# Od, gd and hg stores issued by the sync engine, and every second gd copy staged in a `wn` tile, in a hybrid encoder layer

## The chip, the cores and the metric

The kernel runs on one core of a Trainium2 chip. The metric is the device time of the whole program in microseconds (us): the median of several executions. The engines are TensorE (PE; PEld is its weight load), VectorE (DVE), ScalarE (ACT), GpSimd (POOL) and SyncE (SP). SP computes nothing here; it issues DMA transfers. ACT computes and issues transfers too. Every engine takes its own instructions in order.

## The reference

One layer of an encoder, for 2048 rows of 1024 columns. Cut to its core:

```python
u = rms_norm(h); proj = u @ w_in                   # 1024 -> Hyena, mLSTM, gate columns
hy = short_conv(proj[hyena columns])
y_hy = group_norm(hyena(hy, spectra of the sin-FFN filters))   # two FFT convolutions, gated
qk = silu(short_conv(proj[q, k columns]))
y_ml = group_norm(sigmoid(o_pre) * (mlstm(q, k, v, gates) + mlstm of the flipped rows))
h = h + concat(y_hy, y_ml) @ w_out
q, k, v = norm(h) @ wq, norm(mem) @ wk, norm(mem) @ wv         # mem: 256 rows
h = h + (softmax(q k^T / 16) v per head) @ wo                   # 4 heads of 256
h = h + square(relu(norm(h) @ w1)) @ w2                         # 1024 -> 4096 -> 1024
out = norm(h)
```

## The kernel before

All products are made in single precision by a split: each operand becomes a high and a low part, and `mm3` (L355) issues three matmuls, hi*hi, hi*lo and lo*hi. PE therefore has 14287 matmuls.

The program is written as Python generators, one for each part, and `program` (L2078) weaves them: it steps one generator or the other by the weights that they yield. The order so written goes to a tile framework, which lists the instructions for each engine anew by a timeline that it models (`schedule_with_timeline_sim`). So the order on an engine follows from the order of the code, from the tiles and from the modelled times. A tile is taken by a tag; a tag has a number of buffers (`bufs`), and a tile of the tag can only be written when what used that buffer is done. For a store that means that the data have left the tile.

Every DMA that SP or ACT issues counts on one of eight semaphores in turn, shared by both engines. An issuing instruction waits until the earlier DMA on its semaphore is complete, and then what stands behind it on its engine waits too.

The stages in time, with the generators that make them:

- 0 to some 1030 us: the input projection and the two FFT convolutions of Hyena. `sweep` makes column blocks whose rows are turned; `natural` (L856) makes the blocks of v (`c2` 0 and 1, stored to `vd`) and of the output gate (`c2` 2 and 3, stored to `od`), for each half `hf` of the rows, in eight tiles of 128 rows. After its matmuls a tile is copied by ACT (L885) or passed through a sigmoid by ACT (L887) into a tile `st` of three buffers, and stored (L888). The order of the blocks is: half 1 with blocks 3, 0, 1, 2; half 0 with block 3, later 0 and 1, and at the end block 2.
- some 1020 to 1180 us: `memproj` (L689), woven with the last Hyena transforms and the first mLSTM steps. It folds the attention's weights with the memory rows: `project` (L698) makes `kt`, 16 matmuls (L704) and a copy by ACT (L706); `keys` (L714) makes from `kt` and a weight four products of 128x512 (L721), and each goes through `staged` (L709), a copy by ACT (L711) into a tile `o` of the tag `st`, and a store to `gd` (L723); `values` (L725) does the like for `vw` (L733, L735). There are four `keys` and four `values`. The weights `wm` come through `raw_stream` (L417) on SP in tiles of the tags `wl` and `wh`. The Hyena tail beside it reads `zg` and `hy` (`a`, L963, L966), stores `yh` (L1058) and loads `cbn` (L1248), on SP.
- some 1180 to 1840 us: cross-attention (four chunks `c` of 512 rows), with the remaining mLSTM steps woven in. Its first PE work is L1460, transposes of `wn` tiles that hold `yh`. At the end of a chunk `store` (L1600) scales a block of the result by ACT (L1602) into `hg`, two buffers, and stores it to DRAM (L1603), eight for each chunk.
- from some 1840 us: the MLP, to the end.

An mLSTM step on PE is a chain: updates of the state (L1190), scores (L1274), sums over values and state (L1312 and L1314), with DVE and ACT work between them (L1196, L1284, L1326).

The tag `wn` in the pool of the first stages has four buffers. It holds weights as they land, before they are split (L396).

Of the kernel before, what the change touches and what calls it, by code (L numbers as in the profile page):

```python
# [10 lines left out]
F32 = mybir.dt.float32  # L11
# [122 lines left out]
class Prog:  # L134
# [554 lines left out]
    def memproj(self):  # L689
        nc, sb = self.nc, self.isb  # L690
        gd = self.dram("gd", (2, 128, 8, 512))
        vw = self.dram("vw", (4, 128, 8, 256))
        self.pop(2)
        mt = self.memt

        mul = nc.tensor.matmul

        def project():  # L698
            w = next(self.mst)
            p = self.mm().rearrange("p (k t) -> p k t", k=2)  # L700
            for m in range(2):
                ms = slice(128 * m, 128 * m + 128)
                for k in range(8):
                    mul(p[:, m], w[:, k, ms], mt[k // 4][:, k % 4], start=k == 0, stop=k == 7)  # L704
            t = sb.tile([128, 4, 256], F32, tag="xn", name="kt", bufs=2)[:, 0:2]
            nc.scalar.copy(t, p)  # L706
            return t

        def staged(p):  # L709
            o = sb.tile([128, 2, 256], F32, tag="st", name="o", bufs=3)  # L710
            nc.scalar.copy(o, p)  # L711
            return o

        def keys(h, t):  # L714
            q = next(self.mst)
            for i2 in range(4):
                p = self.mm().rearrange("p (i t) -> p i t", i=2)
                for i in range(2):
                    ds = slice(256 * i2 + 128 * i, 256 * i2 + 128 * i + 128)
                    for m in range(2):  # L720
                        mul(p[:, i], q[:, m, ds], t[:, m], start=m == 0, stop=m == 1)  # L721
                cs = slice(256 * (h % 2), 256 * (h % 2) + 256)
                nc.scalar.dma_start(out=gd[h // 2, :, 2 * i2:2 * i2 + 2, cs], in_=staged(p))  # L723

        def values(h, t):  # L725
            o_ = next(self.mst)
            for mt in range(2):
                ms = slice(128 * mt, 128 * mt + 128)
                for d in range(2):
                    ds = slice(512 * d, 512 * d + 512)  # L730
                    p = self.mm()
                    for m in range(2):
                        mul(p, t[:, m, ms], o_[:, m, ds], start=m == 0, stop=m == 1)  # L733
                    o = staged(p.rearrange("p (i t) -> p i t", i=2))
                    nc.scalar.dma_start(out=vw[2 * d:2 * d + 2, :, 2 * h + mt].rearrange("i p c -> p i c"), in_=o)  # L735

        t = project()
        for i in range(8):
            yield 11
            nxt = project() if i < 7 else None  # L740
            (keys if i < 4 else values)(i % 4, t)
            t = nxt
# [113 lines left out]
    def natural(self, hf, tiles, after=None, at=4):  # L856
        nc, a, sb = self.nc, self.a, self.isb
        xh, xl = self.xh, self.xl
        win = a["w_in"][0]
        for c2 in tiles:  # L860
            n = 256 if c2 < 3 else 272
            c0 = 2560 + 256 * c2
            wh, wl = next(self.wst)
            for t in range(8):
                if t % 4 == 0:
                    yield 11
                if c2 == tiles[-1] and after is not None:
                    if after is True and t == 0:
                        nxt = self.x_chunks(0)
                    if t == at:  # L870
                        if after is True:
                            self.prepq = nxt
                        else:
                            after()
                ts = slice(128 * t, 128 * t + 128)
                r0 = 1024 * hf + 128 * t
                p = self.mm()
                for k in range(8):
                    self.mm3(p[:, :n], xh[:, k, ts], xl[:, k, ts], wh[:, k, :n], wl[:, k, :n], k == 0, k == 7)
                if self.pending:  # L880
                    self.pending.pop(0)()
                self.pop()
                so = sb.tile([128, 512], F32, tag="st", name="st", bufs=3)[:, 0:256]
                if c2 < 2:
                    nc.scalar.copy(so, p[:, :256])  # L885
                else:
                    nc.scalar.activation(so, p[:, :256], AF.Sigmoid)  # L887
                nc.scalar.dma_start(out=(self.d_vd if c2 < 2 else self.d_od)[r0:r0 + 128, 256 * (c2 % 2):256 * (c2 % 2) + 256],  # L888
                                  in_=so)
                if c2 == 3:  # L890
                    sg = sb.tile([128, 16], F32, tag="sg", name="sg", bufs=2)
                    nc.vector.tensor_tensor(sg, p[:, 256:272], self.gb, ALU.add)
                    nc.sync.dma_start(out=self.d_gt[r0:r0 + 128], in_=sg)
# [524 lines left out]
    def attention(self, es):  # L1418
        nc, tc, a = self.nc, self.tc, self.a
        ys = [self.dram("yh", (L, CH)), self.dram("ym", (L, CH))]  # L1420
        gd = self.dram("gd", (2, 128, 8, 512))
        vw = self.dram("vw", (4, 128, 8, 256))
        h2 = self.dram("h2", (4, 128, 8, 512))
        hgd = self.dram("hg", (4, 128, 8, 512))
# [20 lines left out]
        def gemm(w, i, r, p=None, ks=range(8)):  # L1445
            p = p or self.mm()
            ms = slice(128 * i, 128 * i + 128)
            for k in ks:
                self.mm3(p, w[0][:, k, ms], w[1][:, k, ms], r[0][:, k], r[1][:, k], k == 0, k == 7)
            return p  # L1450
# [32 lines left out]
        for c in range(4):  # L1483
# [19 lines left out]
            for ct in range(8):  # L1503
# [14 lines left out]
                if c == 0 and ct < 4:  # L1518
                    p = gemm(w, ct % 2, y, half[ct], range(4, 8))
                else:  # L1520
                    p = gemm(w, ct % 2, y)
# [10 lines left out]
            o = self.act()  # L1532
# [64 lines left out]
            def keep(ct, c=c):  # L1597
                nc.sync.dma_start(out=h2[c, :, ct - 3:ct + 1], in_=acc[:, ct - 3:ct + 1])

            def store(ct):  # L1600
                hg = A.tile([128, 512], F32, tag="hg", name="hg", bufs=2)
                nc.scalar.activation(hg, acc[:, ct], AF.Copy, scale=gf[:, ct:ct + 1])  # L1602
                nc.scalar.dma_start(out=hgd[c, :, ct], in_=hg)  # L1603
                if ct == 3 or (ct == 7 and c < 3):
                    keep(ct)

            for ct in range(8):
                yield 5.2
                if ct % 2 == 0:
                    w = next(wst) if ct else w  # L1610
                else:
                    k = sums.pop(0) if sums else None
                    if k is not None:
                        self.sums_x(A, k, "e")
                if c == 3 and ct in (1, 3, 5):
                    self.ffn_pre(ct // 2)
                if c == 3 and ct in (4, 6):
                    self.load_w1(ct // 2 - 2)
                if c == 3 and ct == 6:
                    x7 = self.ffn_xload(0, 7)  # L1620
                p = gemm(w, ct, o, half[ct], range(4, 8)) if ct < 2 else gemm(w, ct % 2, o)
                if prev is not None:
                    finish(ct - 1, prev, ssum)
                    store(ct - 1)
                prev = p
            if c == 3:
                self.ffn_x(7, x7)
            finish(7, prev, ssum)
            store(7)

            def stats(c=c, ssum=ssum):
# [539 lines left out]
```

## Time and profile before

| | us |
|---|---|
| three runs | 3091.53, 3103.35, 3098.87 |
| their median | 3098.87 |
| the profiled execution, its own time | 3097.53 |
| its span, first to last instruction | 3095.8 |
| mean granted PE clock of the span | 0.992 of full speed |

The profile page's list of DMA queues shows the two queues that hardware feeds, SP's (q1) and ACT's (q10), with packets, MB and the share of the 16 DMA engines' time:

```profile
q1 hardware_dynamic: 405988, 546.54, 55.1%
q10 hardware_dynamic: 37892, 57.79, 5.5%
```

In the prediction's windows the columns are the stretch in us from the start of the span, its length, the busy time of PE, PEld, DVE, ACT and POOL with the number of instructions, the PE clock that was granted (1.00 is full), the busy share of the DMA engines and GB/s. A line of waits has engine, tile, line, the arrow to what released it, the total in us, how many, and the longest. SPq and ACTq are the engines' DMA-issuing instructions. The line numbers are those of the kernel before; from the edit of `staged` on, the changed kernel's are larger by three.

### The profile page before, as it was taken

To read this page: it belongs to the slowest core of one execution; us is meant where nothing else is said; L and a number is where in the kernel's file an instruction comes from. 1 tells how busy PE (TensorE), PEld (TensorE's weight loads), DVE (VectorE), ACT (ScalarE), POOL (GpSimd) and SP (SyncE) were. 2 spreads that over 40 slices of the span, in tenths; PEclk is the share of its full clock that TensorE was granted. 3 is DMA by queue.
4 is the path that set the end of the run, shared out by engine and by line. 5 is a ranking of instruction groups with operands and counts; after the bars stand their busy time and mean duration, and the time that the engine had idled before them with its cause. 6 is when DMAs were issued, how large, how long until landed. Compare 5 with 4: busy or idle time off the path is not lost.

```text
span 3095.8 us, 42982 instructions
## 1 busy us (share of the span) xinstructions
PE 3023.0 (98%) x14287; PEld 2375.2 (77%) x14287; DVE 1952.6 (63%) x3442; ACT 1500.4 (48%) x2930; POOL 1130.9 (37%) x798
## 2 busy tenths in 40 slices
PE   9999999999999998999999999999999999999998
PEld 7655767776676766888887888888888888888876
DVE  8855465446656456877664666557555686566695
ACT  6443465534656225565544455556555543333335
POOL 0122011200222343333132237766466374244653
PEclk9999999999999999999999999999999999999999
DMA  6554767575867997464476556657544565353434
GB/s 225 187 191 164 243 214 237 178 234 193 260 199 241 301 309 231 151 204 160 149 246 222 183 188 224 210 180 240 196 153 151 183 212 171 109 166 117 159 102 164
DMA packets 444102, 607.07 MB, mean 196 GB/s; under 512 B 38494, under 2 KB 248542, under 8 KB 442856
## 3 DMA queue, kind: packets, MB, share of 16 engines
q1 hardware_dynamic: 405988, 546.54, 55.1%
q10 hardware_dynamic: 37892, 57.79, 5.5%
q8 instruction: 113, 1.85, 0.2%
q14 instruction: 109, 0.89, 0.1%
HBM read 401.79 MB, written 202.41 MB: 195 GB/s over the span
## 4 chain that ended last, share of the span: by engine, by line
PE 82%; DMA 7%; DVE 5%; ACT 2%; issue 2%; POOL 1%; SPq 0%; ACTq 0%; DVEq 0%; POOLq 0%
PE mm L357 17%; PE mm L361 17%; PE mm L360 17%; PE hy L357 6%; PE hy L361 6%; PE hy L360 6%; PE hy L178 3%; PE mm L948 2%; PE hy L979 1%; PE hy L1021 1%; DMA a<-hy 1%; DMA xt<-in_x_t_dram 1%; PE hy L1312 1%; PE mm L733 1%; PE hy L1314 1%
## 5 line engine op out<-in xcount | busy, mean ns | idle before, releaser
L1669 ACT CAST ah<-w 128x512 fp32r<-128x512 f32 x284 | 177.1, 624 | 302.0 <-PE hy L360 155.3
L1670 DVE TENSOR_TENSOR bl<-wr,bh 128x512 fp32r<-128x512 f32 x213 | 238.2, 1123 | 124.7 <-ACT bh L1669 124.7
L368 DVE TENSOR_TENSOR wl<-wn,wh 128x512 fp32r<-128x512 f32 (+1 forms) x296 | 215.4, 773 | 101.1 <-ACT wh L368 100.8
L1026 POOL TENSOR_TENSOR b<-b,a 128x512 f32<-128x512 f32 x64 | 86.8, 1359 | 510.5 <-ACT b L1024 240.8
L357 PE MATMUL mm<-xh,wh 128*128 128x512 f32 x640 | 265.5, 416 | 2.5 <-ACT st L206 1.3
L360 PE MATMUL mm<-xl,wh 128*128 128x512 f32 x640 | 252.9, 395 | 1.8 <-DVE xl L368 1.8
L361 PE MATMUL mm<-xh,wl 128*128 128x512 f32 x640 | 253.6, 397 | 0.0
L1670 DVE TENSOR_TENSOR al<-w,ah 128x512 fp32r<-128x512 f32 x236 | 216.4, 917 | 57.1 <-ACT ah L1669 56.9
L1669 ACT CAST bh<-wr 128x512 fp32r<-128x512 f32 x232 | 143.8, 622 | 223.6 <-PE mm L361 173.8
L361 PE MATMUL mm<-bh,al 128*128 128x512 f32 x576 | 223.7, 391 | 3.8 <-DVE al L1670 3.8
L357 PE MATMUL mm<-bh,ah 128*128 128x512 f32 x576 | 225.8, 392 | 0.8 <-DVE acc L1832 0.7
L360 PE MATMUL mm<-bl,ah 128*128 128x512 f32 x576 | 224.9, 390 | 0.0
L368 ACT CAST wh<-wn 128x512 fp32r<-128x512 f32 (+1 forms) x296 | 165.0, 619 | 104.6 <-PE mm L361 52.6
L360 PE MATMUL mm<-act,wh 128*128 128x512 f32 x512 | 201.8, 394 | 0.0
L361 PE MATMUL mm<-act,wl 128*128 128x512 f32 x512 | 199.3, 391 | 0.4 <-DVE wl L368 0.4
L357 PE MATMUL mm<-act,wh 128*128 128x512 f32 x512 | 198.7, 394 | 1.0 <-ACT wh L368 0.9
L357 PE MATMUL hy<-bh,ah 128*128 128x512 f32 x448 | 175.2, 391 | 0.0
L360 PE MATMUL hy<-bl,ah 128*128 128x512 f32 x448 | 174.6, 390 | 0.0
L361 PE MATMUL hy<-bh,al 128*128 128x512 f32 x448 | 174.4, 390 | 0.0
L357 PEld LDWEIGHTS mm<-xh,wh 128*128 128x128 f32 x640 | 120.1, 188 | 56.0 <-issue 19.2
L357 PE MATMUL mm<-wh,xh 128*128 128x256 f32 (+1 forms) x512 | 155.6, 304 | 3.5 <-ACT xh L368 2.0
L361 PEld LDWEIGHTS mm<-xh,wl 128*128 128x128 f32 x640 | 120.1, 188 | 46.2 <-issue 21.8
(380 smaller groups left out, 8219.6 us busy)
## 6 DMA issues: line engine op xcount, KB each, us to landing
wr<-hc SPq DMA_DIRECT2D x224, 256.0 KB
w<-in_ff_w_dram SPq DMA_DIRECT2D x172, 256.0 KB
hc<-wn SPq DMA_DIRECT2D x128, 256.0 KB
wn<-in_w_in_dram SPq DMA_DIRECT2D x100, 256.0 KB
hc<-q SPq DMA_DIRECT2D x96, 256.0 KB
fs<-a SPq DMA_DIRECT2D x32, 512.0 KB
a<-fs SPq DMA_DIRECT2D x64, 256.0 KB
a<-zs SPq DMA_DIRECT2D x64, 256.0 KB
```

The lines of the kernel that those rows point to most:

```text
L178: b = self.nc.tensor.matmul(*products[-1], start=True, stop=True)
L357: first = mm(ps, lh, rh, start=start, stop=False)
L360: mm(ps, lh, rl, start=False, stop=False)
L361: self.last = mm(ps, ll, rh, start=False, stop=stop)
L368: both = (self.nc.scalar.copy(hi, src), self.nc.vector.tensor_tensor(lo, src, hi.bitcast(F32), ALU.subtract))
L733: mul(p, t[:, m, ms], o_[:, m, ds], start=m == 0, stop=m == 1)
L948: nc.tensor.matmul(pp, dm[:, m], t[:, m], start=True, stop=True)
L979: nc.tensor.matmul(pg, em[:, m], y, start=True, stop=True)
L1021: nc.tensor.matmul(pp, dm[:, m], t[:, m], start=True, stop=True)
L1026: nc.gpsimd.tensor_tensor(xt, xt, hi[:, m], ALU.mult)
L1669: self.nc.scalar.copy(hi, src)
L1670: eng.tensor_tensor(lo, src, hi.bitcast(F32), ALU.subtract)
```

## The change

Three groups of stores are issued by `nc.sync` (SP) instead of `nc.scalar` (ACT): the `od` stores of column block 2 in `natural` (16), the `gd` stores of `keys` (16) and the `hg` stores of attention (32). The `od` stores of block 3, the `vd` stores and the `vw` stores stay on ACT. In `keys`, the copies of `i2` 0 and 2 go to a tile of the tag `wn` (four buffers), those of 1 and 3 to the tag `st` (three) as before. The bytes and the arithmetic are the same.

```diff
-        def staged(p):
-            o = sb.tile([128, 2, 256], F32, tag="st", name="o", bufs=3)
+        def staged(p, wide=False):
+            if wide:
+                o = sb.tile([128, 2, 256], F32, tag="wn", name="o", bufs=4)
+            else:
+                o = sb.tile([128, 2, 256], F32, tag="st", name="o", bufs=3)
             nc.scalar.copy(o, p)
             return o
...
-                nc.scalar.dma_start(out=gd[h // 2, :, 2 * i2:2 * i2 + 2, cs], in_=staged(p))
+                nc.sync.dma_start(out=gd[h // 2, :, 2 * i2:2 * i2 + 2, cs], in_=staged(p, i2 % 2 == 0))
...
-                nc.scalar.dma_start(out=(self.d_vd if c2 < 2 else self.d_od)[r0:r0 + 128, 256 * (c2 % 2):256 * (c2 % 2) + 256],
-                                  in_=so)
+                (nc.sync if c2 == 2 else nc.scalar).dma_start(
+                    out=(self.d_vd if c2 < 2 else self.d_od)[r0:r0 + 128, 256 * (c2 % 2):256 * (c2 % 2) + 256], in_=so)
...
-                nc.scalar.dma_start(out=hgd[c, :, ct], in_=hg)
+                nc.sync.dma_start(out=hgd[c, :, ct], in_=hg)
```

How the scheduler lists the instructions now, at the places that matter. First ACT in the keys' stage, before, with the semaphores that a row waits for (DMAHW0 to DMAHW7 are the eight DMA semaphores; a name like PE_49 is an engine's own):

```order
L723 DMA gd<-o 128x2x256 [waits DMAHW5_49,Activation_49]
L711 COPY o<-mm 128x512 [waits DMAHW3_49,PE_49]
L1184 ACTIVATE ve<-va,cols 128x129 [waits DMAHW7_49]
L1184 ACTIVATE ve<-va,cols 128x129 x3
L723 DMA gd<-o 128x2x256 [waits DMAHW6_49,Activation_49]
L711 COPY o<-mm 128x512 [waits DMAHW1_49,PE_49]
L723 DMA gd<-o 128x2x256 [waits DMAHW1_49,Activation_49]
L213 ACTIVATE brm<-ms,eps 128x16 [waits DVE_49]
L706 COPY kt<-mm 128x512 [waits PE_49]
```

and of the change:

```order
L714 COPY o<-mm 128x512 [waits PE_49]
L1187 ACTIVATE ve<-va,cols 128x129 [waits DMAHW7_49]
L1187 ACTIVATE ve<-va,cols 128x129 x3
L714 COPY o<-mm 128x512 [waits PE_49]
L714 COPY o<-mm 128x512 [waits DMAHW3_49,PE_49]
L213 ACTIVATE brm<-ms,eps 128x16 [waits DVE_49]
L706 COPY kt<-mm 128x512 [waits PE_49,Activation_49]
```

The stores and their waits on DMA semaphores have left ACT; of the copies one in this piece still waits for a DMA, that of its own tile. `kt` (L706) stands behind no store.

SP in the same stage, before:

```order
L417 DMA wm<-in_xa_wk_dram 128x4x256 x2
L1248 DMA cbn<-cbd 128x516 x2
L1058 DMA yh<-a 64x1024 x2
L417 DMA wm<-in_xa_wq_t_dram 128x1024 x2
L963 DMA a<-zg_2632 128x1024 x2
L966 DMA a<-hy 64x1024 x2
L417 DMA wm<-in_xa_wv_dram 128x4x256 x2
```

and of the change:

```order
L417 DMA wm<-in_xa_wk_dram 128x4x256 x2
L726 DMA gd<-o 128x2x256 x2
L1251 DMA cbn<-cbd 128x516 x2
L726 DMA gd<-o 128x2x256
L1061 DMA yh<-a 64x1024 x2
L726 DMA gd<-o 128x2x256
L417 DMA wm<-in_xa_wq_t_dram 128x1024 x2
L966 DMA a<-zg_2632 128x1024 x2
L969 DMA a<-hy 64x1024 x2
L417 DMA wm<-in_xa_wv_dram 128x4x256 x2
L726 DMA gd<-o 128x2x256 x2
```

The `gd` stores stand between the loads of `wm`, `cbn`, `a` and the stores of `yh`.

PE at the passage from the memory projection to attention (`...` stands for the L1312 and L1314 rows of a step), before:

```order
L733 MATMUL mm<-wm,kt 128x512 x4
...
L1190 MATMUL hy<-ve,kn 128x129 x4
L1274 MATMUL hy<-qn,kk_t 128x128 x4
...
L1190 MATMUL hy<-ve,kn 128x129 x4
L1460 MATMUL hy<-ident,wn 128x128 x16
```

and of the change:

```order
L736 MATMUL mm<-wm,kt 128x512 x4
...
L1193 MATMUL hy<-ve,kn 128x129 x4
L1277 MATMUL hy<-qn,kk_t 128x128 x4
...
L1193 MATMUL hy<-ve,kn 128x129 x4
L1277 MATMUL hy<-qn,kk_t 128x128 x4
...
L1193 MATMUL hy<-ve,kn 128x129 x4
L1463 MATMUL hy<-ident,wn 128x128 x16
```

Between the last product of the memory projection and the first transposes of attention there is now one mLSTM step more.

## The prediction

> **What bounds the kernel now.** First the page's shares of busy time and its chain of waits, then the TensorE idle time by stretches of the span, then the waits inside the stretches that the change touches.
>
> ```profile
> span 3095.8 us, 42982 instructions
> PE 3023.0 (98%) x14287; PEld 2375.2 (77%) x14287; DVE 1952.6 (63%) x3442; ACT 1500.4 (48%) x2930; POOL 1130.9 (37%) x798
> PE 82%; DMA 7%; DVE 5%; ACT 2%; issue 2%; POOL 1%; SPq 0%; ACTq 0%; DVEq 0%; POOLq 0%
> ```
>
> TensorE (PE) is busy 98% of the span: 3095.8 - 3023.0 = 72.8 us is all its idle time, and no change to stores can win more than that and what the clock loses around it. ACT, which issues the stores now, is busy 48%, so freeing it is worth something only where PE stands behind it. The windows say where that can be (columns: us, PE, PEld, DVE, ACT and POOL busy with counts, granted PE clock, DMA share, GB/s):
>
> ```profile
> 990.00:1010.00 20.00, 15.63 (x86) 11.55 (x86) 10.20 (x19) 10.64 (x17) 6.21 (x5) 0.91 0.64 200
> 1050.00:1110.00 60.00, 53.11 (x226) 39.63 (x225) 25.75 (x70) 10.60 (x23) 17.89 (x13) 0.94 1.05 362
> 1110.00:1130.00 20.00, 17.61 (x86) 11.96 (x85) 10.93 (x36) 7.11 (x22) 10.77 (x9) 1.00 1.05 376
> 1180.00:1210.00 30.00, 18.63 (x109) 16.98 (x108) 24.37 (x70) 16.81 (x59) 10.24 (x8) 0.77 0.86 287
> 1400.00:1500.00 100.00, 100.00 (x550) 86.45 (x549) 75.90 (x207) 52.71 (x166) 29.41 (x22) 1.00 0.41 128
> ```
>
> The first row holds the end of the second batch of od stores, the second and third the gd stores of the keys, the fourth the passage from the memory projection to attention, the fifth is inside attention, where the hg stores lie: PE has no hole there at all. Now where the stores sit:
>
> ```profile
> L888 ACTq DMA_DIRECT2D od<-st x32: 326/327/696, 500.9 to 1023.4; - x32
> L723 ACTq DMA_DIRECT2D gd<-o x16: 366/366/435, 1053.2 to 1128.3; - x16
> L1603 ACTq DMA_DIRECT2D hg<-hg x32: 326/326/442, 1353.1 to 1839.5; - x32
> ```
>
> **Part 1, the key stores (gd), the largest term.** In ACT's own order a gd store stands between two copies, and it can be held there: what comes behind it on ACT waits too. ACT's waits from 1045 to 1125 us put that down to loads that have nothing to do with ACT's data:
>
> ```profile
> ACT brm L213 <- DMA a<-hy: 12.1, 3, 4.4
> ACT o L711 <- DMA wm<-in_xa_wq_t_dram: 11.0, 4, 7.2
> ACT o L711 <- DMA wm<-in_xa_wo_dram: 10.6, 1, 10.6
> ACT brm L213 <- DMA wm<-in_xa_wo_dram: 10.2, 1, 10.2
> ```
>
> One of them in full, with PE beside it (timeline: start, us, engine, line, operation, count, idle before and releaser):
>
> ```profile
> 1055.37 0.57 ACT L711 COPY o<-mm 128x512 f32<-128x512 f32 x1
> 1059.64 0.37 ACTq L723 DMA_DIRECT2D gd<-o  x1
> 1060.27 0.57 ACT L706 COPY kt<-mm 128x512 f32<-128x512 f32 x1
> 1060.89 5.37 PE L721 MATMUL mm<-kt,wm 128*128 128x256 f32 x16 [2.83 <-ACT kt L706]
> ```
>
> The copy ended at 55.94, the store left at 59.64: ACT, with nothing else to do, stood 3.7 us at the store. `kt`, which PE needs for the next head, was copied only behind it, and PE stood 2.83 us. Its sixteen matmuls then took 5.37 us. The same sixteen for the head before:
>
> ```profile
> 1054.34 3.72 PE L721 MATMUL mm<-kt,wm 128*128 128x256 f32 x16 [0.79 <-ACT o L711]
> 1060.00:1070.00 10.00, 7.25 (x25) 4.66 (x25) 4.94 (x16) 1.96 (x4) 3.52 (x3) 0.83 1.05 392
> ```
>
> So the hole cost 2.83 us and then 5.37 - 3.72 = 1.65 us of a lower clock (0.83 granted in these ten microseconds). By the Trainium skill, "TensorE: Matmul & The Clock Gate", section "Part 1: The HAM clock gate", the clock is gated by recent activity and is given back only after some 4 us of sustained matmuls; the row above agrees in kind, with 1.65 us lost behind one hole.
>
> All PE waits of 1045 to 1115 us that the profile names for this stage:
>
> ```profile
> PE mm L721 <- ACT kt L706: 2.8, 1, 2.8
> PE mm L721 <- ACT o L711: 2.2, 2, 1.4
> PE mm L704 <- ACT o L711: 1.9, 1, 1.9
> ```
>
> 2.8 + 2.2 + 1.9 = 6.9 us, and 60 - 53.11 = 6.9 us is the idle time of the window: every hole of the stage is an ACT copy that came late. The clock of 0.94 over 60 us loses another 60 x 0.06 = 3.6 us. With the stores issued from SP, the copies on ACT follow one another without these stops; what can still hold one is its tile. Three `st` tiles were the bound on copies whose stores have not landed; every second copy now goes to one of the four `wn` tiles, so seven tiles carry the sixteen copies. Upper bound of the gain: 6.9 + 3.6 = 10.5 us. Lower bound: none, if the copies now wait for tiles as long as they did for the issue (DMA is full there, share 1.05, so stores land slowly). I take the upper end, **-10.5**, since no wait in these rows is on a tile of the copy itself except 2.0 us:
>
> ```profile
> ACT o L711 <- DMA gd<-o: 2.0, 2, 1.3
> ```
>
> In the stretch behind it (1110 to 1130 us, the last gd stores and the first values) PE idles 20 - 17.61 = 2.4 us at full clock. Values still store from ACT. Between 0 and 2.4 I take **-2**.
>
> What the sixteen stores do on SP: SP issues them among the loads of `wm`, `yh`, `a`, and an SP row that waits for its copy delays what is behind it. SP waits for other engines in any case, and the weights come long before they are needed: `wm` of wo was issued at 1093.10 and first read at 1117.11.
>
> ```profile
> 1093.10 1.01 SPq L417 DMA_DIRECT2D wm<-in_xa_wo_dram  x2
> L733 PE MATMUL mm<-wm,kt x64: 592/592/697, 1117.1 to 1176.5; 128*128 128x512 f32 x64
> ```
>
> 24 us of slack cover a stop of 3.7 us, so I put this at 0; without that cover each stop would cost at most what ACT paid, the 10.5 us won, and the part would come out at 0.
>
> **Part 2, the od stores.** Sixteen of thirty-two leave ACT, eight for each half of the rows. Around the first eight (half 1) PE has no hole, and around the eight of the third column block of half 0, which stay on ACT, it has one:
>
> ```profile
> 610.00:630.00 20.00, 20.00 (x134) 16.64 (x133) 8.57 (x17) 9.02 (x17) 3.22 (x3) 1.00 0.33 98
> 650.00:670.00 20.00, 16.07 (x91) 12.12 (x88) 5.63 (x13) 4.79 (x9) 0.00 (x0) 0.83 1.02 306
> ACT xh L368 <- DMA a<-hy: 8.6, 2, 4.5
> ```
>
> So the first eight are worth 0, and the 20 - 16.07 = 3.9 us of the second row, with ACT's waits of the third, stay as they are: its stores are not among those moved. In the second eight (half 0) one store held ACT:
>
> ```profile
> 987.69 0.39 ACT L887 ACTIVATE st<-mm 128x256 f32<-128x256 f32 x1
> 991.59 0.33 ACTq L888 DMA_DIRECT2D od<-st  x1
> 991.96 0.59 ACT L980 COPY a<-hy 128x512 f32<-128x512 f32 x1 [3.88 <-DMA a<-zs]
> ```
>
> 987.69 + 0.39 = 988.08 to 991.59 is 3.5 us, and the copy behind it opens the next transform of the Hyena path. In 990 to 1010 us PE idles 20 - 15.63 = 4.4 us and the clock of 0.91 loses 20 x 0.09 = 1.8 us, so 0 to 6.2 us are to be had. But some of it is the wait for the data itself (`a<-zs` is named). The stop of 3.5 us is nearest; with some clock I take **-4**.
>
> **Part 3, the hg stores.** Thirty-two issues of 0.33 us are 10.4 us of ACT, in a stage where PE is busy 100.00 of 100 us and ACT 52.7. ACT's wait for a free `hg` tile is small and stays (both tiles stay):
>
> ```profile
> ACT hg L1602 <- DMA hg<-hg: 8.8, 6, 2.6
> ```
>
> Hidden behind PE: 0. If that cover went, 8.8 us is what the tiles could cost once more.
>
> **Part 4, what the scheduler moves.** The memory projection's matmuls go ahead of the mLSTM steps that used to lie between them, so that two steps instead of one stand bare, with no projection work between their matmuls, before attention's first transposes. What a bare step costs shows at the end of the old order:
>
> ```profile
> 1179.67 1.16 PE L1274 MATMUL hy<-qn,kk_t 128*128 128x128 f32 x8 [0.83 <-DVE cf L1196]
> 1193.26 2.09 PE L1190 MATMUL hy<-ve,kn 128*128 128x129 f32 x8 [7.58 <-ACT ht L1326]
> ```
>
> The window 1180 to 1210 us idles 30 - 18.63 = 11.4 us and loses 30 x 0.23 = 6.9 us of clock: 18.3 us for the bare stretch. The second bare step is between 0 (its state is ready early, since the projection no longer delays it, and other work of the weave fits in) and the same 18.3 again. The matmuls are the same in number; what is lost is only the cover, and the attention's loads are issued earlier too. I take **+4**, nearer the lower end, as only 7.58 us of the old stretch is one step's own wait and half of that can be covered by loads and turns that now come a step earlier.
>
> **Sum**, against the profiled execution: 3097.53 - 10.5 - 2 - 4 + 4 = **3085 us**. The median of the three runs, 3098.87, is 1.3 us above it, which I neglect.
>
> **Rivals.**
>
> (1) The new order helps as well. The memory projection ends a step earlier, attention's weights and `yh` loads come earlier, and of the bare stretch's 18.3 us some 8 to 10 go instead of 4 coming: 3097.5 - 10.5 - 2 - 4 - 9 = 3072 us. For it: SP lists the attention loads earlier; PE's one wait there on a load, 4.4 us, would go.
>
> ```profile
> PE hy L1460 <- DMA wn<-yh: 4.4, 1, 4.4
> ```
>
> Against it: the 7.58 us above is a wait on ACT and DVE work of the step, which no load shortens.
>
> (2) Nothing but issue time moves. 16 x 0.33 + 16 x 0.37 + 32 x 0.33 = 22 us leave an engine that is half idle, and the copies wait for the landing of stores as long as they waited to issue: 3097.5 us. For it: DMA share 1.05, so nothing in the stage ends before the bytes are moved. Against it: the quoted store that held `kt` for 3.7 us. The Trainium skill, "DMA: Bandwidth & Descriptors", section "Issuing engines are not separate DMA queues", speaks for this rival: all transfers run on the same 16 engines whoever starts them, and only the time to start them is saved. The trace agrees that this time is small, 0.33 to 0.37 us each, but shows ten times that at single held issues.
>
> (3) Slower: the mLSTM passage decides. The keys' stage is bound by its bytes (362 GB/s at share 1.05), so the copies' gain there is given back at once; the projection's matmuls were the filler of the mLSTM steps, and the second bare step costs the full 18.3 us. 3097.5 + 18.3 = 3116 us. It decides from the point where gains 1 and 2 stay under the price of the step. For it: the fourth window, the worst of all, is exactly such a stretch. Against it: PE's holes in the keys' stage are all behind ACT, none behind DMA.
>
> **How the numbers follow.** Forecast 0.42, rival (1) 0.25, rival (2) 0.10, rival (3) 0.23. The likeliest gives 3085 us. Its own range, from the gd gain at 0 to 10.5 and the bare step at 0 to 12, is 3077 to 3097. To hold 8 in 10 the range takes in most of rivals (1) and (3): 3064 to 3113 us. About what a measurement of this kernel can tell from no change is 0.5%, 15.5 us: below 3083 is faster, above 3114 slower. Of the forecast somewhat under half lies beyond it (0.19), with all of rival (1): faster 0.44. Rival (3) lies beyond on the other side for most of its chance: slower 0.22. The rest, half the forecast and rival (2) and what rival (3) leaves: 0.34.
>
> **What would show it.** Part 1 is right if, in the profile of the changed kernel, ACT's waits on `wm` and `hy` loads in the keys' stage go, PE waits there for L714 and L706 are under 1 us together, and the clock of that window is above 0.98. It is wrong if L714 waits for `gd` landings instead. Part 2: no copy behind L887 stands for `zs`. Part 3: PE is full from 1353 to 1840 us as before. Part 4: the stretch ahead of the first L1463 transposes has two holes of the kind of 7.58 us; if their sum with the clock is above 20 us, rival (3) holds, if the stretch got shorter, rival (1). The forecast falls if PE begins to wait for `wm`, `yh` or `wn` loads, which would mean that SP's stops have become the bound.

## The result: 0.18% slower, and the profile after

The changed kernel takes 3105.34 us (median of 22 runs, 3099.75 to 3110.86) against 3100.89 us for the kernel before (22 runs). The ratio is 1.0018, 95% interval 1.0012 to 1.0024: 5.6 us slower by the ratio, where 12.5 us less were forecast. It is inside the bound that was named as no change, and the interval, 3.7 to 7.4 us, leaves out zero. The medians are 4.5 us apart, which lies inside the interval too.

The head of the page of the profiled execution after (span, busy time of each engine, shares of the chain of waits, the two hardware queues):

```profile
span 3101.0 us, 43002 instructions
PE 3025.5 (98%) x14287; PEld 2378.3 (77%) x14287; DVE 1947.7 (63%) x3442; ACT 1497.5 (48%) x2930; POOL 1132.0 (37%) x798
PE 82%; DMA 7%; DVE 6%; ACT 2%; issue 2%; POOL 1%; SPq 0%; ACTq 0%; DVEq 0%; POOLq 0%
q1 hardware_dynamic: 417252, 561.23, 56.9%
q10 hardware_dynamic: 26628, 43.10, 4.1%
```

The change did what it says: 14.7 MB moved from ACT's queue (57.79 to 43.10 MB) to SP's. The span grew by 5.2 us. Where, the windows show. The keys' stage, the values and the passage to attention, before (columns as in the prediction):

```profile
1040.00:1110.00 70.00, 63.11 (x271) 46.98 (x270) 27.14 (x72) 12.37 (x28) 22.90 (x17) 0.95 1.05 352
1110.00:1165.00 55.00, 52.61 (x238) 35.97 (x237) 29.07 (x91) 21.69 (x74) 26.42 (x20) 1.00 0.84 283
1165.00:1225.00 60.00, 47.64 (x273) 39.46 (x272) 41.74 (x131) 32.43 (x111) 19.75 (x15) 0.89 0.76 248
```

and after, with the second od stretch ahead and the stage of the hg stores behind:

```profile
990.00:1010.00 20.00, 16.88 (x96) 12.66 (x96) 9.34 (x19) 10.30 (x17) 5.85 (x5) 0.91 0.60 194
1040.00:1110.00 70.00, 66.89 (x293) 49.58 (x292) 28.45 (x73) 15.05 (x33) 26.87 (x19) 0.98 1.07 348
1110.00:1165.00 55.00, 52.11 (x210) 33.16 (x209) 24.27 (x75) 17.79 (x54) 18.23 (x14) 0.97 0.86 280
1165.00:1225.00 60.00, 39.92 (x227) 35.10 (x226) 39.12 (x138) 31.15 (x115) 23.05 (x19) 0.80 0.68 224
1350.00:1850.00 500.00, 498.10 (x2446) 416.48 (x2445) 326.39 (x679) 255.41 (x605) 154.05 (x109) 1.00 0.58 193
```

What a window loses is its idle time and, of its busy time, the share that the clock was short. Keys: before 6.9 + 63.11 x 0.05 = 10.0 us, after 3.1 + 66.89 x 0.02 = 4.4 us: 5.6 us won. Values: 2.4 before, 2.9 + 52.11 x 0.03 = 4.5 after: 2.1 lost. Passage: 12.4 + 47.64 x 0.11 = 17.6 before, 20.1 + 39.92 x 0.20 = 28.1 after: 10.5 lost. Sum: 7.0 us lost in these 185 us; the rest of the span gives some 2 us back (the clock is a rounded figure, so the sum is no better than 1 to 2 us).

PE's waits from 980 to 1260 us in the changed kernel, the four longest and the one on a weight:

```profile
PE hy L1315 <- DVE bry L218: 9.5, 1, 9.5
PE hy L1193 <- ACT ht L1329: 5.4, 3, 2.9
PE hy L1463 <- DVE act L368: 4.8, 1, 4.8
PE hy L178 <- DMA a<-zg: 2.6, 2, 2.3
...
PE mm L724 <- DMA wm<-in_xa_wq_t_dram: 0.8, 2, 0.5
```

The waits of the key products for ACT, 6.9 us before, are gone (no L704 or L724 wait on ACT). What PE still waits for in the keys' stage are loads: 2.6 us for `zg` and 0.8 us for `wm`, where before 0.3 us were for `zg`. A new wait of 9.5 us stands in the passage. The same shows in the times of two places, the last value product (the tile's row) and attention's first transposes (the timeline), of the changed kernel:

```profile
L736 PE MATMUL mm<-wm,kt x64: 592/592/697, 1108.3 to 1166.1; 128*128 128x512 f32 x64
1199.56 0.66 PE L1463 MATMUL hy<-ident,wn 128*128 128x128 f32 x4 [0.70 <-DVE cf L1199]
```

and the first transposes of the kernel before:

```profile
1195.14 2.58 PE L1460 MATMUL hy<-ident,wn 128*128 128x128 f32 x12
```

The last value product starts 10.4 us earlier than before (1176.5 there), and attention starts 4.4 us later (1195.14 there).

### The profile page after: what moved, and what is told of

Same layout as the page of the kernel before. It is cut to its first block, busy times and chain, and to the rows that moved or that the text cites. A ratio compares the mean times of both kernels' runs of the same rounds, so it can differ in the third digit from the quotient of the medians.

```text
span 3101.0 us, 43002 instructions
## 1 busy us (share of the span) xinstructions
PE 3025.5 (98%) x14287; PEld 2378.3 (77%) x14287; DVE 1947.7 (63%) x3442; ACT 1497.5 (48%) x2930; POOL 1132.0 (37%) x798
## 3 DMA queue, kind: packets, MB, share of 16 engines
q10 hardware_dynamic: 26628, 43.10, 4.1%
## 4 chain that ended last, share of the span: by engine, by line
PE 82%; DMA 7%; DVE 6%; ACT 2%; issue 2%; POOL 1%; SPq 0%; ACTq 0%; DVEq 0%; POOLq 0%
PE mm L357 17%; PE mm L361 17%; PE mm L360 17%; PE hy L360 6%; PE hy L361 6%; PE hy L357 6%; PE hy L178 3%; PE mm L951 2%; PE hy L982 1%; PE hy L1024 1%; DMA a<-hy 1%; DMA xt<-in_x_t_dram 1%; PE hy L1315 1%; DMA gd<-o 1%; PE hy L1317 1%
## 5 line engine op out<-in xcount | busy, mean ns | idle before, releaser
L1673 DVE TENSOR_TENSOR bl<-wr,bh 128x512 fp32r<-128x512 f32 x213 | 238.6, 1125 | 126.8 <-ACT bh L1672 126.8
```

The costliest lines, as they stand in the source:

```text
L1673: eng.tensor_tensor(lo, src, hi.bitcast(F32), ALU.subtract)
```

## The experiments

Fourteen kernels, in four sets; those of a set ran on one chip with the kernel before. Each diff is against the kernel before or against the change, as said.

**Which part loses.** Four kernels: the key stores with both their edits, the SP issue alone, the `wn` tile alone, and all but the key stores.

`gd_alone` (against before: the `staged` edit of the change, and)

```diff
-                nc.scalar.dma_start(out=gd[...], in_=staged(p))
+                nc.sync.dma_start(out=gd[...], in_=staged(p, i2 % 2 == 0))
```

> The key stores on SP with every second copy in a wn tile; od and hg as before. Theory O (the order lost it): PE has the changed order at the passage to attention (two bare mLSTM steps) and freed copies in the keys' stage; nearly all of the change's loss is here, 3 to 6 us above before, and PE waits ahead of the first transposes as long as in the full change (a hole of 9 us). Theory S (stores on SP delay the loads behind them): also 3 to 6 us above, but PE or ACT waits on loads. Theory H (od or hg lost it): 5 to 10 us below before, ratio 0.997 to 0.998.

Measured: 1.0019 (1.0010 to 1.0028), the whole loss of the change, so theory H is out. In its profile PE waits 9.3 us at L1315 in the passage, as theory O has it. It also waits 4.0 us for `zg` and 1.0 us for `wm`; the next two kernels tell theory O from theory S.

`gd_st_tiles` (against before)

```diff
-                nc.scalar.dma_start(out=gd[...], in_=staged(p))
+                nc.sync.dma_start(out=gd[...], in_=staged(p))
```

> The key stores on SP, all copies in st tiles as before. Theory O: PE keeps the old order with one bare step, ACT is freed of the held stores; some 5 to 10 us below before (ratio 0.997 to 0.998), the keys' stage idles under 3 us. Theory S: as slow as the full change or slower, 3 to 8 us above before, since the same sixteen stores stand among the loads. If the three st tiles bind, it is at before within 2 us and ACT's copies wait on gd landings.

Measured: 0.9997 (0.9988 to 1.0006): neither faster nor slower; the third case of the expectation. Its waits, ACT's from 1030 to 1125 us and PE's from 1000 to 1210 us:

```profile
ACT o L711 <- DMA gd<-o: 42.4, 8, 9.8
```

```profile
PE mm L721 <- ACT o L711: 6.2, 2, 5.4
PE mm L704 <- ACT o L711: 4.2, 2, 3.9
```

ACT's copies now wait 42.4 us for the landing of an earlier `gd` store, that is for one of three `st` tiles; before that was 2.0 us. PE waits 10.4 us for these copies, as against 6.9 us; of the 3.5 us more, 2.4 come back in the values' window, where PE now has no idle time. The stop at the store's issue was only the first of two doors; with it open, the waiting is done at the tile.

`wide_act` (against before: the `staged` edit, and)

```diff
-                nc.scalar.dma_start(out=gd[...], in_=staged(p))
+                nc.scalar.dma_start(out=gd[...], in_=staged(p, i2 % 2 == 0))
```

> The key stores on ACT as before, every second copy in a wn tile. Theory O: the wide tile alone gives PE the changed order; the held stores stay; the second bare step costs and little is won, 5 to 15 us above before. Theory S: within 2 us of before, as no store has moved to SP.

Measured: 1.0023 (1.0014 to 1.0032). No store has moved to another engine, and the loss is all there, against theory S. The order of PE's 14287 matmuls is in this trace, row for row, that of `gd_alone`: it is the tiles that change it. In its keys' stage PE still waits 6.4 us for ACT's copies, so the SP issue alone (10.4 us) and the tiles alone (6.4 us) leave the waits standing; only both together take them away.

`no_gd` (against before: the od and hg lines of the change)

> The od stores of block 2 and the hg stores on SP, the key stores as before. Theories O and S: within 3 us of before, at best the 1.2 us that the stretch 900 to 1000 us won. Theory H: 3 to 8 us above before.

Measured: 0.9998 (0.9989 to 1.0007). These 48 stores are worth nothing that could be told from zero. The window of the second od stretch and the waits of PE in it:

```profile
990.00:1010.00 20.00, 15.72 (x106) 12.99 (x104) 8.30 (x19) 9.82 (x16) 5.81 (x5) 1.00 0.71 223
```

```profile
PE hy L979 <- DVE b L1027: 2.7, 1, 2.7
PE hy L1021 <- DVE b L1025: 1.7, 1, 1.7
```

ACT no longer stops there: its copy L980 stands right behind the sigmoid, at 988.76 instead of 991.96. PE's idle time is 20 - 15.72 = 4.3 us, as before (4.4): the next thing that it waits for is DVE's `b`, and that was as late. The clock is better in this window (1.00 for 0.91) and worse in the next 20 us (0.91 for 1.00), and the time of the whole is the same. One window can't price so little: in three kernels whose od stores were left alone, `gd_alone`, `wide_act` and `gd_st_tiles`, PE idles 2.9 to 4.4 us in it.

**Which tiles.** `wn` tiles for the first two or the last two key heads alone, all key stores on SP:

```diff
-                ... in_=staged(p, i2 % 2 == 0))
+                ... in_=staged(p, i2 % 2 == 0 and h < 2))     # gd_h01;  h > 1 in gd_h23
```

> Key stores on SP; every second copy in a wn tile for the first two key heads alone, st tiles for the other two. PE has one bare mLSTM step ahead of attention, as before. Theory O (the order at the passage lost what the tiles won): the holes of the first two heads go, the passage stays: 4 to 8 us below before, ratio 0.9974 to 0.9987. Rival T (wide tiles themselves, by the traffic that they let through, cost): 3 us or more above before. Rival N (the tiles win nothing, as the stage is bound by its transfers, and only the passage matters): within 2 us of before.

> As the run before, with the wn tiles for the last two heads alone. PE has two bare steps ahead of attention, nearly as in the full change. Theory O: 3 to 8 us above before, with the hole of 9 us at L1315. Rival T: as gd_h01. Rival N: 5 to 10 us above before.

Measured: `gd_h01` 0.9991 (0.9982 to 1.0000), `gd_h23` 1.0036 (1.0024 to 1.0049). The same number of tiles, the same stores, and 0.45% apart. The scheduler leaves one bare mLSTM step ahead of attention in the first and two in the second. Passage windows, `gd_h01` and then `gd_h23`:

```profile
1165.00:1225.00 60.00, 47.90 (x273) 40.16 (x273) 39.82 (x120) 31.12 (x108) 19.63 (x16) 0.86 0.74 237
```

```profile
1165.00:1225.00 60.00, 39.55 (x222) 33.01 (x220) 37.23 (x130) 31.09 (x112) 21.18 (x17) 0.80 0.72 238
```

`gd_h23` loses 20.5 + 39.55 x 0.20 = 28.4 us there, as the full change does; `gd_h01` 12.1 + 47.90 x 0.14 = 18.8, near the 17.6 of before. In its keys' stage `gd_h01` has most of what the full change won (66.03 of 70 us busy at clock 0.98), but in the values' window it loses 7.5 us, where before lost 2.4. So its gain, 2.8 us by the ratio, is less than the 4 to 8 that theory O expected, and the three windows do not place it. `gd_h23` loses 11 us, more than theory O (3 to 8) or rival N (5 to 10) gave it; its holes at L1315 are two, of 6.8 and 5.0 us, and not one of 9. Rival T asked for a loss of 3 us or more in both, and `gd_h01` has none: the same number of tiles costs nothing there.

**Taking a bare step out of the stage.** One mLSTM piece less beside the projection, so one more in attention:

```diff
-                             p.turned_in(), take(n, 2), beside_each(n, take(m, 5)))
+                             p.turned_in(), take(n, 2), beside_each(n, take(m, 4)))
```

> The kernel before with four mLSTM pieces instead of five beside the memory projection: one step more goes into the attention, where PE is full. The bare step of the old passage goes: theory O, 12 to 18 us below before (ratio 0.994 to 0.996), if a bare step costs what the window showed, 18.3 us less the 5 us of its own matmuls. If a bare step costs little, or the step is only paid for later, within 3 us.

> The full change with four mLSTM pieces instead of five: one bare step is left ahead of attention, not two. Theory O: 10 to 18 us below the full change, so 5 to 13 us below before (ratio 0.996 to 0.998). If the second bare step isn't the loss, within 4 us of the full change (ratio 1.001 to 1.003).

Measured: 1.0039 (1.0026 to 1.0053) for the kernel before so edited, 1.0039 (1.0026 to 1.0051) for the change: both slower, against both lines of the expectation. PE's waits in the first, from 1000 to 1500 us:

```profile
PE hy L1460 <- DMA wn<-ym: 8.7, 2, 7.8
PE hy L1460 <- DMA wn<-yh: 6.2, 1, 6.2
```

With one step less, attention's first transposes are reached before their data (`yh`) are loaded, and later transposes wait 8.7 us for the mLSTM's result (`ym`), for which the kernel before waits 0.2 us. In the second kernel the hole at L1315 stays (9.4 us) and the wait for `ym` is 7.2 us. So the bare steps aren't idle ballast: what follows needs them. This pair cannot price a bare step.

**What stands in the 9.5 us hole.** The chain of waits of the changed kernel, from PE's end of the step before (1168.08) to the product that PE needs:

```profile
1168.57 0.74 SPq L1252
1169.41 5.14 DMA kn<-kn
1174.67 0.97 ACT ve L1187 x3
1175.65 2.07 ACT wh L368 x4
1177.71 1.19 ACT junk L1342 x8
1178.92 0.31 ACT brm L213
...
1180.99 1.28 DVE rw L1287 x2
```

A load of 5.1 us, ACT's `ve`, the casts of `we` (the weights that the attention stage uses first), the norm of an earlier step, DVE's `rw`. Three kernels move single groups of rows of this stretch, by an order dependence that adds no semaphore. `after_ve_late`, against the change:

```diff
+                if r == 12:
+                    behind(ve copy, norm of the second step)
```

> The full change, with one group of four ACT copies (ve of the fourth mLSTM step) put behind the norm of the second step, two rows later on ACT; SP and DVE in the same order. Theory Q: the hole of 9.5 us ahead of L1315 is a queue in order, va and kn loads that leave SP only when PE ends the step before, then ve, the casts of we, the norm and the rw product behind them; without ve at the head the casts of we start at about 1172 instead of 1175.6 us, the hole shrinks to 5 to 7 us and the time falls by 2 to 5 us against the full change (ratio to before 1.000 to 1.0012). Rival Z (the hole is the price of a bare step, whatever stands at the head): the hole stays over 8.5 us and the ratio at 1.0015 to 1.0022.

`after_we_b2` and `before_we_b2`, against the change and the kernel before:

```diff
+                behind(DVE wl <- we, the rw product of the step)
```

> The full change, with the four DVE rows wl<-we of attention's first weights put behind the rw product. Theory Q: DVE waited for ACT's norm in any case (it came 0.5 us behind the four rows), so the hole stays at 8 to 9.5 us and the time within 2 us of the full change. If these four rows are the head of the queue, the hole falls under 6 us and the time by 3 us or more.

> The kernel before, with the same four DVE rows put behind the rw product. In the old order they stood ahead of den, for which PE waited 7.58 us at L1190. Theory Q: that hole falls to 2 to 5 us and the time by 3 to 6 us (ratio 0.998 to 0.999). Rival Z: the hole and the time stay (within 1.5 us).

Measured: `after_ve_late` 1.0017 (1.0008 to 1.0026), `after_we_b2` 1.0027 (1.0018 to 1.0036), `before_we_b2` 0.9998 (0.9989 to 1.0007). PE's waits in the passage, one fence for each, in that order:

```profile
PE hy L1320 <- DVE bry L220: 7.2, 1, 7.2
...
PE hy L1198 <- ACT ht L1334: 3.8, 2, 3.4
```

```profile
PE hy L1315 <- DVE bry L218: 9.5, 1, 9.5
```

```profile
PE hy L1190 <- ACT ht L1326: 7.6, 1, 7.6
```

With `ve` behind the norm the hole is 2.3 us shorter (7.2), the next wait is 1.3 us longer (3.8 for the 2.5 that the change has there), and the time does not fall. The four DVE rows are not the head of the queue, neither after, as expected, nor before, where 2 to 5 us of the 7.6 were expected to remain and all did. So neither of the two groups that were moved makes the hole. That it is the length of one step's chain, where a row taken out uncovers the next, fits this and the chain above; it is not shown, since the load of 5.1 us, the longest piece, was not moved.

`gd_h01_we_b2`: `gd_h01` with the same four rows moved.

> Key stores on SP, wn tiles for the first two heads alone (3.7 us below before when run by itself), and the four DVE rows put behind the rw product. Theory Q: both add up, 6 to 10 us below before (ratio 0.9968 to 0.998). Rival Z: as without the move, 2 to 5 us below before.

Measured: 0.9986 (0.9977 to 0.9995), 3096.16 us. It has the lowest ratio here, and the only interval that lies wholly below 1; the 6 to 10 us of theory Q are not reached. The rows' move adds nothing that could be told from `gd_h01` (0.9991), and the order of PE's matmuls is the same in both; what they share is `wn` tiles for the first two heads.

**Putting the cover back.** All tiles and stores of the change; only the eight products of the last value head are put behind the update of the third mLSTM step (`cover_20`) or of the second (`cover_10`):

```diff
+                        if h == 3:
+                            behind(value product, last update matmul of the step)
```

> The full change with the eight products of the last value head put behind the update of the third mLSTM step: one step is left without cover, as before. Theory O (the order is the loss): some 7 us of products lie in the holes again, 4 to 9 us below the full change, so within 4 us of before or under it (ratio 0.9985 to 1.0008), and the 9.5 us hole is gone or under 5 us. Rival T (the tiles and their traffic): no gain, ratio 1.0012 or more.

> As cover_20, behind the update of the second step: two bare steps stay behind the products. Theory O: little changes against the full change, ratio 1.001 to 1.0025, with a hole over 6 us in the bare steps. Rival T: the same ratio, so only together with cover_20 does it tell: if both are at 1.000 it is not the bare steps but the place of the products as such.

Measured: `cover_20` 1.0012 (1.0003 to 1.0021), `cover_10` 1.0006 (0.9997 to 1.0015). PE's waits in the passage (timeline), `cover_20` and then `cover_10`:

```profile
1173.10 0.77 PE L1321 MATMUL hy<-va,rw 128*128 128x129 f32 x2 [3.08 <-DVE bry L218]
...
1202.85 3.01 PE L1469 MATMUL hy<-ident,wn 128*128 128x128 f32 x12 [6.18 <-DMA wn<-yh]
```

```profile
1183.48 2.09 PE L1196 MATMUL hy<-ve,kn 128*128 128x129 f32 x8 [6.07 <-ACT ht L1335]
...
1196.55 0.65 PE L1469 MATMUL hy<-ident,wn 128*128 128x128 f32 x4 [0.71 <-DVE cf L1205]
```

In `cover_20` the 9.5 us hole is down to 3.1, but the loads of `yh` now leave SP later (from 1200.1 us, in the change from 1173.4), and the first transposes wait 6.2 us. The time did not fall as theory O had it (1.0008 or less); 1.0012 is the bound that stood for rival T. In `cover_10`, expected to change little, the 9.5 us hole is gone, one of 6.1 stands, and attention starts at 1196.55 for the change's 1199.56. By the point estimates it takes back two thirds of the loss (0.0012 of 0.0018), with the tiles untouched; the two intervals overlap, and theory O expected this of `cover_20` and not of `cover_10`. So the pair supports the order as the cause and does not show it.

**One bare step or two.** The loss in the passage's window (1165 to 1225 us), worked out as above, with the mLSTM steps that PE has in each trace between the last value product and attention's first transposes:

| kernel | bare steps | PE busy (us of 60), clock | lost, us | ratio |
|---|---|---|---|---|
| before | 1 | 47.64, 0.89 | 17.6 | 1 |
| `gd_st_tiles` | 1 | 47.28, 0.89 | 17.9 | 0.9997 |
| `no_gd` | 1 | 47.79, 0.89 | 17.5 | 0.9998 |
| `gd_h01` | 1 | 47.90, 0.86 | 18.8 | 0.9991 |
| the change | 2 | 39.92, 0.80 | 28.1 | 1.0018 |
| `gd_alone` | 2 | 40.03, 0.80 | 28.0 | 1.0019 |
| `wide_act` | 2 | 39.99, 0.80 | 28.0 | 1.0023 |
| `gd_h23` | 2 | 39.55, 0.80 | 28.4 | 1.0036 |
| `cover_10` | 2 | 46.10, 0.83 | 21.7 | 1.0006 |

Whatever the engine that stores, the second bare step goes with some 10 us more in this window, but for `cover_10`. The four kernels with moved rows fall in line (17.4 and 18.4 us with one step, 27.4 and 28.5 with two). `after_take4` does not: it has one bare step, keeps the hole of 9.4 us and loses 29.2 us, 7.2 of them to the wait for `ym`. In all kernels of the table two bare steps come together with `wn` tiles for the last two heads, so the table alone does not part the order from those tiles; `cover_10` is the one that leaves the tiles and fills a hole.

## Why the prediction was wrong, point by point

**The keys (forecast -10.5).** The step that failed is the choice of the upper end, "since no wait in these rows is on a tile of the copy itself except 2.0 us". The copies had not waited for tiles because they were held at the issue ahead of it. `gd_st_tiles` shows it: 42.4 us of tile waits come up where 2.0 stood, and the time is that of before. The SP issue by itself measured 0.9997, the lower end of the bound. With the `wn` tiles too, the stage did lose the holes behind ACT: 5.6 us of the 10.5 by the windows above. So the term was mis-sized by half, and it needs the tiles as well as the SP issue. The other half is idle time that is left, 3.1 us, most of it waits for loads, and the clock, 0.98 over the window. Of the signs named for this part, ACT's waits on `wm` and `hy` and PE's waits on the copies are gone; but copies do wait for `gd` landings (7.7 us), which was named as the sign against it, without PE waiting for them.

**The passage (forecast +4).** This is the term that turned the sign. The step was taken "nearer the lower end", with half of a step's wait covered by earlier loads. The windows show 10.5 us. In the trace the loads of the bare step do not run ahead: SP issues `va` when PE ends the step before, at 1167.9, and `cbn` and `kn` behind it, to 1169.4; the last of them holds the chain for 5.1 us. The value products that were PE's work during such a chain lie ahead of it now. The prediction's upper end, 18.3 us, counted the clock over idle time as well; over the busy time it is 11.4 + 18.63 x 0.23 = 15.7. (The clock terms of the keys and the od stores have the same slip, by some 0.4 us each.)

Rival (3) named this mechanism, the place and the sign; its price was too high, since it gave the keys no gain at all: 5.6 were won and 10.5 + 2.1 lost. That the tiles bring the loss, and not the engine that stores, is shown (`wide_act` against `gd_st_tiles`). That they do it through the order rests on `gd_h01` and `gd_h23` (the same number of tiles, other heads, 0.45% apart, one and two bare steps) and is supported by `cover_10`. What a bare step costs apart from what stands around it stays open: taking one away moved the waits on to `yh` and `ym`.

**The values (forecast -2).** They lost 2.1, with one PE wait of 2.9 us at L1193 among them, where the mLSTM steps stand closer.

**The od stores (forecast -4).** Nothing that could be measured. The stop of ACT was there and is gone, PE's idle time is the same: in `no_gd` DVE's `b` came as late as ACT's copy had. The step that failed is "the stop of 3.5 us is nearest": the stop of an engine was priced in place of the wait of PE. PE's own waits from 985 to 1015 us in the kernel before, which the prediction didn't read, put 3.2 of 4.4 us down to DVE's `b`:

```profile
PE hy L1021 <- DVE b L1025: 2.1, 1, 2.1
PE hy L1190 <- ACT a L980: 1.2, 1, 1.2
PE hy L979 <- DVE b L1027: 1.1, 1, 1.1
```

**The hg stores (forecast 0).** Right: PE is busy 498.10 of 500 us there, 497.89 before, and `no_gd` is at 0.9998.

**The stores on SP (forecast 0).** Right as far as these traces go. PE does wait 3.4 us for `wm` and `zg` in the changed kernel, as against 0.3 us. But the loads did not leave SP later: the `zg` load that PE waits longest for went out at 1064.18, before at 1064.80, and PE came to it at 1074.18 instead of 1080.51. PE caught up with the loads; the stores did not push them back.

**Rival (2)**, with the Trainium skill's rule from "DMA: Bandwidth & Descriptors", section "Issuing engines are not separate DMA queues", that another issuing engine saves only the time to start a transfer: true of all 64 stores as far as the issue goes (0.9997 for the keys' sixteen, 0.9998 for the others). It was given 0.10, too little for that part; its time, no change, did not come either, since it has no term for the order.

**The range.** The range given to the forecast by itself, 3077 to 3097, does not come out of its own bounds: with 3097.53 - 2 - 4 = 3091.5, the keys at -10.5 to 0 and the step at 0 to 12 it is 3081 to 3104.

## What to carry to other kernels

An engine that stands at a store's issue is one door; look for the next one behind it, the buffer that the store holds, before pricing the wait: here the wait moved whole from the issue to the tile. Where a scheduler lists the work, more buffers in one stage also change the order in the next; find the work that lay in the holes of a long chain and see whether it still does. And price a stop of an engine by what the engine that sets the end waits for, not by how long the stop is.

## What was not expected of the hardware

Opening the keys' stage did not load the DMA engines further: their share from 1040 to 1110 us was 1.05 before and 1.07 after, at 352 and 348 GB/s. PE's 3.8 us more of busy time there (63.11 to 66.89) came at the same rate of transfer: a share that reads as full did not mean that PE's work there was bound by the bytes. What PE then waited for, 3.4 us, was single loads.
